# The low parts of weight blocks, formed by an accumulating DMA onto the negated high part

## The chip, the cores and the metric

The kernel runs on one core of one Trainium2 chip. The metric is the device time of one execution in microseconds (us); smaller is better. The engines are named as in the profile: PE (TensorE; PEld is its weight load), DVE (VectorE), ACT (ScalarE), POOL (GpSimd) and SP (SyncE, which issues most DMAs).

## The reference

One step of a two-layer streaming model, in float32, for a prompt of 512 tokens and a sample of 32 tokens, of width 1024. In both layers the normed input goes through `w_mix_in`; 256 of its columns query a memory of 256 rows, and the other 768 go through a state space mixer (S5, 48 groups of 64 states) in layer 0 and through latent attention with 12 heads in layer 1. Both parts go through `w_mix_out` and are added to the stream. A feed-forward part with a short convolution follows.

```python
for layer in range(DEPTH):                                     # DEPTH = 2
    z = rms_norm(h, norm_mix_g[layer]) @ w_mix_in[layer]
    z_mix, z_mem = z[..., :MIX_IN], z[..., MIX_IN:]            # 768 and 256 columns
    mem_out = memory_attend(rms_norm(z_mem...), mem_k[layer], mem_v[layer])
    mix_out = s5_mixer(z_mix, ...) if layer == 0 else mla_attention(...)
    h = h + concatenate([mix_out, mem_out]) @ w_mix_out[layer]
    h = h + conv_ffn(rms_norm(h, norm_ffn_g[layer]), ...)      # 1024 -> 5632 -> 2816 -> 1024
```

The memory's keys and values of the prompt are computed for both layers by `w_mem_kv` (`memory_kv`). The outputs are the stream, these keys and values, the new latents and rotary keys, and the final states of S5 and of the convolution.

## The kernel before, in words

The stream lies feature-major in `h[0..7]`, 128 features by 544 columns (512 of the prompt, 32 of the sample). Float32 products are made from float32r parts: an operand x is split into a high part `hi` (x rounded by a copy) and a low part `lo` = x - `hi`, and a product is `hi*hi + hi*lo + lo*hi`. `gemm` and `gemm_part` (L322) issue these three for a block of 128 output features, in two halves of 272 columns: 8 slices of 128 input features give 48 matmuls per block of 128x1024 weights, 6 slices give 36 per block of 128x768.

A weight block comes through `weights` (L227 to L233). SP loads it into `wraw` (L229), ACT copies it to `whi` (L230), and POOL subtracts into `wlo` (L231). Where a caller passes `lo_eng=V`, DVE subtracts: the four blocks of `mem_kv` for layer 1, and two of the three blocks of `kv_group`. `wraw`, `whi` and `wlo` have three buffers each, handed out in turn; the buffers of a block come back when PE has done its last matmul on it (`wfree`), and `wraw` when the low part is formed. So the high part of a block starts when PE ends the block three places earlier. 186 blocks come this way. The first two blocks of layer 0 (`weights_part`, L240) and the nine blocks of `w_uq` (L1284) make their low parts by code of their own.

The program runs in this order: the first product of layer 0 (`z0`) with the parameters of S5 (`s5_params`, L532 to L660); the S5 stage, six steps in which DVE and POOL form matrices (`s5_wv` L668 to L670, `s5_wc` L695 to L706), DVE scans (`s5_scan`, L761 to L779) and the eight blocks of `mem_kv` (matmuls at L348) go along as filling; the memory's attention and the gated product of layer 0; `mix_out`; `ffn` of layer 0; the same for layer 1 with the latent attention instead of S5. In `ffn` each pair of blocks gives two halves of the convolution: `conv` takes the product out of PSUM on DVE (L842 to L844), copies context columns on POOL (L846, L847), scales on ACT (L849) and adds on DVE (L850, L851). `down` multiplies back. Ahead of `ffn` and of layer 1 stands a norm: `norm_stat` sums squares on PE (L258, L260), `rsqrt` (L249 to L253) works on DVE, `norm_bcast` transposes on PE (L282).

A scheduler orders the instructions of each engine when the program is built, and engines run their own lists in order.

Of the kernel before, what the change touches and what calls it, by code (L numbers as in the profile page):

```python
# [9 lines left out]
F32 = mybir.dt.float32  # L10
F32R = mybir.dt.float32r
I32 = mybir.dt.int32
AF = mybir.ActivationFunctionType
ALU = mybir.AluOpType
# [47 lines left out]
# by how many instructions a unit moves ahead in the order of issue  # L62
# [15 lines left out]
class Slots:  # L78
    """Fixed buffers handed out in turn; the order of reuse is the order of the trace."""
# [38 lines left out]
    def retire(self, *tiles):  # L118
        """the buffers on these tiles are not handed out again"""
        self.gone |= {t[:].tensor.name for t in tiles}  # L120
        self.free = [t for t in self.free if t[:].tensor.name not in self.gone]
# [16 lines left out]
def body(ctx, tc, A, O):  # L138
# [29 lines left out]
    def sm(n, name, bufs=2):  # L168
        """small tiles: per name a ring of fixed buffers"""
        ring = small.setdefault((name, n), [[], 0])  # L170
        if len(ring[0]) < bufs:
            ring[0].append(base.tile([128, n], F32, name=f"{name}{n}_{len(ring[0])}"))
            return ring[0][-1]
        ring[1] += 1
        return ring[0][(ring[1] - 1) % bufs]

    # ---- constants and small parameters
# [36 lines left out]
    # ---- helpers  # L214
# [4 lines left out]
    def split_parts(po, smp):  # L219
        """high and low parts of a block given by its prompt and sample columns"""  # L220
        hi, lo = R.get(NT), R.get(NT)
        for c, x in ((slice(0, NP), po), (slice(S0, NT), smp)):
            S.activation(hi[:, c], x, AF.Copy)
            V.tensor_tensor(lo[:, c], x, hi[:, c].bitcast(F32), ALU.subtract)
        return hi, lo

    def weights(ap, *n, lo_eng=None):  # L227
        raw, hi, lo = WR.get(*n), WH.get(*n), WL.get(*n)
        nc.sync.dma_start(raw, ap)  # L229
        S.activation(hi, raw, AF.Copy)  # L230
        (lo_eng or P).tensor_tensor(lo, raw, hi.bitcast(F32), ALU.subtract)  # L231
        WR.put(raw)
        return hi, lo  # L233

    def weights_part(w, ap, c, lo_eng):
        """part of a weight block, ready on its own"""
        raw, hi, lo = (a[:, c] for a in w)
        nc.sync.dma_start(raw, ap[:, c])
        S.activation(hi, raw, AF.Copy)
        lo_eng.tensor_tensor(lo, raw, hi.bitcast(F32), ALU.subtract)  # L240
# [25 lines left out]
    def norm_stat(accs, bs):  # L266
        """1/rms per token from partial sums of squares [128, NT], tokens on the partitions"""
        ps = bs.get(512)
        if len(accs) == 2:
            V.tensor_tensor(accs[0], accs[0], accs[1], ALU.add)  # L270
        stat_cols(accs[0], ps)
        F.put(*accs)
        x = sm(5, "nx")
        V.tensor_scalar(x, ps[:, :5], 1.0 / D, EPS, ALU.mult, ALU.add)  # L274
        bs.put(ps)
        return rsqrt(x, 128, 5, "nr")

    def norm_bcast(r, bs):
        """the same along the columns on all partitions"""
        pa, pb = bs.get(512), bs.get(512)  # L280
        for t in range(4):
            T.transpose(pa[:, 128 * t:128 * t + 128], r[:, t:t + 1].to_broadcast([128, 128]), ident)  # L282
        T.transpose(pb[:, :NS], r[:NS, 4:5].to_broadcast([NS, 128]), ident[:NS, :NS])  # L283
        rb = F.get(NT)
        V.tensor_copy(rb[:, :NP], pa)
        V.tensor_copy(rb[:, S0:], pb[:, :NS])
        bs.put(pa, pb)
        return rb
# [21 lines left out]
    def gemm(ps, xs, w):  # L310
        """feature layout product of one block of 128 features: psum pair = w^T x"""
        for k in range(len(xs)):
            gemm_part(ps, xs, w, k, len(xs))
        wfree(w)
# [16 lines left out]
    # ---- memory keys and values of the prompt, both layers  # L331
# [85 lines left out]
    # ---- attention to the memory  # L417
    def mem_attend(l, zm, kv_p, kv_s, fm, bm, out):
# [25 lines left out]
        # sample: the 4 heads' queries side by side on the partitions  # L444
# [81 lines left out]
    # ---- S5: partitions hold two groups of 64 states (groups 8m+i and 8m+4+i), columns the 24 pairs  # L526
    NPR = 4 * NM

    def s5_exp(pool, x, name):
        """exp of a small tile to float32 accuracy"""  # L530
        k, r, y, e = (pool.tile([128, NPR], F32, name=f"{name}{i}") for i in "kry2")
        V.tensor_scalar(x, x, -87.0, 88.0, ALU.max, ALU.min)  # L532
        V.tensor_scalar(k, x, 1.0 / math.log(2.0), MAGIC, ALU.mult, ALU.add)
        V.tensor_scalar(k, k, MAGIC, None, ALU.subtract)
        V.scalar_tensor_tensor(r, k, -LN2_HI, x, ALU.mult, ALU.add)
        V.scalar_tensor_tensor(r, k, -LN2_LO, r, ALU.mult, ALU.add)
        V.tensor_scalar(e.bitcast(I32), k, 127.0, 8388608.0, ALU.add, ALU.mult)
        V.tensor_scalar(y, r, 1.0 / 5040, 1.0 / 720, ALU.mult, ALU.add)
        V.tensor_tensor(y, y, r, ALU.mult)
        for c in (120, 24, 6, 2, 1):  # L540
            V.scalar_tensor_tensor(y, y, 1.0 / c, r, ALU.add, ALU.mult)
        V.scalar_tensor_tensor(y, y, 1.0, e, ALU.add, ALU.mult)
        return y

    def s5_params(pool, tmp, sp5):
# [16 lines left out]
        # angles of the powers 1, 8, 16, ..., 512  # L562
# [28 lines left out]
        # input factor (lambda - 1) / a  # L591
# [16 lines left out]
        def cm(o, n, a, b):  # L608
            """powers o..o+n-1 = power a times powers b..b+n-1"""
# [10 lines left out]
        # b scaled by the input factor: -im, re, im  # L620
# [7 lines left out]
        # unit rotations by 8 theta at chunk positions 0..64, then 0..4 again  # L628
# [14 lines left out]
        # the same with the real and imaginary parts on the partitions  # L643
# [18 lines left out]
    def s5_wv(q, m, fs):  # L662
        """per group the map of a chunk's input to the state, [128 (step, channel), (re, im), pair, 128]"""
# [23 lines left out]
    def s5_wc(q, m, fs, bs):  # L687
        """per group the map of the state to the chunk's output, and the kernel within the chunk, written to DRAM"""
# [23 lines left out]
    def s5_kernel(q, m, fs):  # L712
        """the kernel within the chunk in its Toeplitz form"""
# [8 lines left out]
    def s5_input(zt, fs, bs):  # L722
        """zt [128, 552], tokens in chunks of 8 -> [128 (step, channel), 8 groups, 69 chunks], last step first"""
# [20 lines left out]
    def s5_scan(q, m, u, wv, fs, bs):  # L744
        """states before each chunk [128, (re, im), 4 pairs, 70]: 0..63 prompt, 64 its end, 65..68 sample, 69 its end.
        The state turns by 8 theta per chunk: in the turning frame both parts follow a real recurrence"""
# [63 lines left out]
    # ---- shared layer parts  # L810
    def mix_out(l, xs, rs, bs):
        """h += w_out^T xs; sums of squares for the next norm"""
# [94 lines left out]
    # ---- layer 0  # L907
# [11 lines left out]
    # the first two blocks part by part as their data comes in  # L919
# [83 lines left out]
    R, fx = slots(lr, 4, F32R, 512, "rb"), slots(lr, 14, F32, FW, "fx")  # L1003
# [5 lines left out]
    # units of the memory's keys and values that go along with each step  # L1009
# [100 lines left out]
    # ---- layer 1  # L1110
# [19 lines left out]
    # query latent (gain applied, scale deferred) and memory queries  # L1130
# [42 lines left out]
    # per column (4 tiles x 4 heads of the prompt, the sample) the scale of the query latent, its square over the widths  # L1173
# [6 lines left out]
    # latent and rotary key of the new tokens  # L1180
# [23 lines left out]
    def finish_latents():  # L1204
# [39 lines left out]
        # the rotary key, three times on the partitions: high, high, low parts  # L1244
# [28 lines left out]
    # queries: per group of 4 heads the projections, then norms, rotation and transposes  # L1273
# [82 lines left out]
    def absorb(g, qa):  # L1356
        """the sample's queries taken to the latent's side of the key projection; the rotary part high, low, high"""
# [18 lines left out]
    # norms of the keys of the cache and of the new tokens of the sample  # L1376
# [34 lines left out]
    # scores of the sample against all its keys, keys on the partitions, before the rotary part  # L1411
# [21 lines left out]
    def sample_attend(g):  # L1433
        """weights of the sample for four heads, the sum of its latents, the values from it"""
# [19 lines left out]
        # each part has its own maximum: factors that bring the parts together, over the sum  # L1454
# [43 lines left out]
    # keys and values of the prompt for a group  # L1498
# [49 lines left out]
    def prompt_scores(qt, kt):  # L1548
        """one head: weights, 4 query tiles in 3 buffers"""
# [20 lines left out]
    def prompt_values(prs, vt, h0, smp):  # L1570
        """the two heads of a pair side by side on the output's partitions"""
# [40 lines left out]
    def run(*gens):  # L1612
        """units of several streams in turn"""
        gens = list(gens)
        while gens:
            gens = [(k, g) for k, g in gens if unit(k, g) is not g]
# [44 lines left out]
    # how many units of the memory's attention go along with each round  # L1661
# [52 lines left out]
def arrays(a):  # L1714
# [44 lines left out]
    def pairs(v):  # L1759
        """[48 groups, 64 states, ...] -> [128 (half, state), 24 pairs, ...]"""  # L1760
        v = v.reshape((NM, 2, 4) + v.shape[1:])
        v = np.moveaxis(v, (1, 3), (0, 1))
        return v.reshape((128, 4 * NM) + v.shape[4:])
# [36 lines left out]
```

## Time and profile before

| | |
|---|---|
| median of 3 runs | 1480.92 us (1479.81 to 1484.13) |
| span of the profiled execution, first to last instruction | 1480.6 us |
| PE busy | 1411.5 us, 95% of the span |
| DVE busy | 876.6 us, 59% |
| ACT busy | 590.8 us, 40% |
| POOL busy | 711.6 us, 48% |
| moved by DMA | 120.49 MB, 81 GB/s on average |

The profiled execution has no separate time beside its span; the span lies 0.3 us under the median of the runs. Busy shares are averages over stages of different kinds, so the rows below are read by stage.

### The profile page before, as it was taken

What the parts mean: (1) busy time and instruction counts of PE and PEld (TensorE: products, weight loads), DVE (VectorE), ACT (ScalarE), POOL (GpSimd) and SP (SyncE); (2) the same over time, 40 slices, a digit from 0 to 9 for tenths busy, and PEclk for the clock granted to TensorE, in tenths of its full rate; (3) what the DMA queues carried; (4) which work ended last, traced back from release to release, by engine and by line L of the source; (5) the groups of instructions that cost most, each with busy time, mean ns of one, the idle gap of its engine ahead of it and who ended that gap; (6) DMA issues with size and microseconds to landing.
All of it is one profiled execution on the core that took longest, in us unless ns stands there. A gap on an engine that the chain in (4) does not pass through costs nothing. (4 is left out here: it accounts for less than half of the span.)

```text
span 1480.6 us, 26541 instructions
## 1 busy us (share of the span) xinstructions
PE 1411.5 (95%) x10693; PEld 1319.2 (89%) x10693; DVE 876.6 (59%) x1807; ACT 590.8 (40%) x1061; POOL 711.6 (48%) x643
## 2 busy tenths in 40 slices
PE   7686789989999999999999999999999999999998
PEld 6675678989999999999998998557999999999998
DVE  8999975177742773265447765673367633772462
ACT  5334455243432332244454554563334422442231
POOL 4647635545544554456636522442635544554442
PEclk9898899999999999999999999999989999999999
DMA  5222222212222222222223230000222222222222
GB/s 209 85 68 74 87 86 73 99 59 86 93 93 86 86 86 87 90 81 89 84 83 98 65 107 29 15 15 15 86 72 86 86 87 86 92 93 87 86 78 86
DMA packets 45115, 120.49 MB, mean 81 GB/s; under 512 B 5152, under 2 KB 14336, under 8 KB 44992
## 3 DMA queue, kind: packets, MB, share of 16 engines
q1 hardware_dynamic: 43008, 114.80, 23.1%
q10 hardware_dynamic: 1152, 2.10, 0.4%
q0 software_dynamic: 832, 1.91, 0.4%
q8 instruction: 84, 1.38, 0.4%
q14 instruction: 39, 0.32, 0.1%
HBM read 113.17 MB, written 5.61 MB: 80 GB/s over the span
## 5 line engine op out<-in xcount | busy, mean ns | idle before, releaser
L322 PE MATMUL bank<-rc,whi 128*128 128x272 f32 x3728 | 632.5, 291 | 5.0 <-DVE rc L303 4.2
L231 POOL TENSOR_TENSOR wlo<-wraw,whi 128x1024 fp32r<-128x1024 f32 (+2 forms) x180 | 421.4, 2341 | 373.8 <-ACT whi L230 368.8
L322 PEld LDWEIGHTS bank<-rc,whi 128*128 128x128 f32 x3728 | 532.8, 190 | 9.2 <-DVE rc L303 5.3
L322 PE MATMUL bank<-rc,wlo 128*128 128x272 f32 x1864 | 389.9, 290 | 0.0
L230 ACT ACTIVATE whi<-wraw 128x1024 fp32r<-128x1024 f32 (+2 forms) x186 | 191.2, 1028 | 411.5 <-PE bank L322 309.7
L322 PEld LDWEIGHTS bank<-rc,wlo 128*128 128x128 f32 x1864 | 294.8, 190 | 0.3 <-issue 0.2
L322 PE MATMUL bank<-g,whi 128*128 128x272 f32 x1408 | 235.2, 289 | 0.0
L850 DVE SCALAR_TENSOR_TENSOR fa<-fa,gp,fa 128x546 f32<-128x546 f32 x88 | 160.1, 1819 | 80.8 <-ACT fa L849 80.8
L322 PEld LDWEIGHTS bank<-g,whi 128*128 128x128 f32 x1408 | 199.3, 188 | 0.5 <-ACT g L216 0.3
L322 PE MATMUL bank<-g,wlo 128*128 128x272 f32 x704 | 146.2, 289 | 0.0
L864 DVE TENSOR_TENSOR h<-bank,h 128x272 f32<-128x272 f32 x96 | 37.8, 435 | 170.8 <-PE bank L322 170.8
L322 PEld LDWEIGHTS bank<-g,wlo 128*128 128x128 f32 x704 | 110.6, 188 | 0.0
L849 ACT ACTIVATE fa<-fa,gp 128x546 f32<-128x546 f32 x88 | 74.4, 845 | 48.2 <-DVE fa L844 48.2
L846 POOL COPY fa<-gp 128x2 f32<-128x2 f32 x88 | 18.6, 212 | 148.6 <-DVE g L217 106.2
L890 ACT ACTIVATE fa<-fa 128x546 f32<-128x546 f32 x44 | 29.1, 662 | 131.0 <-DVE fa L851 131.0
L851 DVE SCALAR_TENSOR_TENSOR fa<-fa,gp,fa 128x546 f32<-128x546 f32 x88 | 69.3, 788 | 3.1
L322 PE MATMUL bank<-ra,whi 128*128 128x272 f32 x256 | 52.3, 328 | 19.7 <-DVE fa L966 8.5
L322 PEld LDWEIGHTS bank<-ra,whi 128*128 128x128 f32 x256 | 43.0, 218 | 22.7 <-DVE fa L966 9.0
L847 POOL COPY fa<-fa 128x4 f32<-128x4 f32 x88 | 56.5, 642 | 11.7 <-DVE fa L844 11.7
L842 DVE TENSOR_TENSOR fa<-bank,fa 128x272 f32<-128x272 f32 x88 | 38.6, 438 | 33.6 <-PE bank L322 31.9
L217 DVE TENSOR_TENSOR g<-fa,g 128x544 fp32r<-128x544 f32 x44 | 37.8, 860 | 31.6 <-ACT g L216 31.6
L891 DVE TENSOR_TENSOR fa<-fa,fa 128x512 f32<-128x512 f32 x44 | 30.5, 693 | 35.1 <-ACT fa L890 35.1
(678 smaller groups left out, 2016.8 us busy)
## 6 DMA issues: line engine op xcount, KB each, us to landing
wraw<-i_w_f SPq DMA_DIRECT2D x120, 512.0 KB
wraw<-i_w_out SPq DMA_DIRECT2D x16, 512.0 KB
wraw<-i_w_in SPq DMA_DIRECT2D x14, 512.0 KB
wraw<-i_w_f SPq DMA_DIRECT2D x16, 384.0 KB
wraw<-i_w_mkv SPq DMA_DIRECT2D x8, 512.0 KB
wraw<-i_w_uq SPq DMA_DIRECT2D x9, 384.0 KB
wraw<-i_w_glu SPq DMA_DIRECT2D x6, 384.0 KB
h<-i_x SPq DMA_DIRECT2D x8, 272.0 KB
```

The costliest lines, as they stand in the source:

```text
L217: V.tensor_tensor(lo, src, hi.bitcast(F32), ALU.subtract)
L230: S.activation(hi, raw, AF.Copy)
L231: (lo_eng or P).tensor_tensor(lo, raw, hi.bitcast(F32), ALU.subtract)
L322: T.matmul(ps[q][:, :c], ww, xx[:, c0:c0 + c], start=k == 0 and i == 0, stop=k == n - 1 and i == 2)
L842: V.tensor_tensor(u[:, 2:274], ps[0][:, :272], rb[:, :272], ALU.mult)
L847: P.tensor_copy(view(cvo, [[2, 2], [1, 2]], 4 * c), view(u, [[34, 2], [1, 2]], 512))
L849: S.activation(y, u[:, 2:548], AF.Identity, scale=gcol("cw", 3 * ci + 2), bias=gcol("cb", ci))
L850: V.scalar_tensor_tensor(y, u[:, 1:547], gcol("cw", 3 * ci + 1), y, ALU.mult, ALU.add)
L851: V.scalar_tensor_tensor(y, u[:, 0:546], gcol("cw", 3 * ci), y, ALU.mult, ALU.add)
L864: V.tensor_tensor(h[m][:, c0:c0 + cc], ps[qd][:, :cc], h[m][:, c0:c0 + cc], ALU.add)
L890: S.activation(yg, yg, AF.Silu)
L891: V.tensor_tensor(u[:, 2:514], ya[:, :NP], yg[:, :NP], ALU.mult)
```

## The change

`weights` forms the low part in two steps. ACT writes the raw block times -1 into `wlo`, which rounds as the high part does, so that `wlo` = -`whi`. Then a DMA that POOL issues reads the block from DRAM a second time and adds it to `wlo` in SBUF. The subtraction on POOL or DVE is gone, and `lo_eng` has no effect. The raw buffer comes back after ACT's second copy. The pool `fx` of the S5 stage has 13 buffers in place of 14. Apart from comments that are taken out, nothing else is changed.

```diff
     def weights(ap, *n, lo_eng=None):
         raw, hi, lo = WR.get(*n), WH.get(*n), WL.get(*n)
         nc.sync.dma_start(raw, ap)
         S.activation(hi, raw, AF.Copy)
-        (lo_eng or P).tensor_tensor(lo, raw, hi.bitcast(F32), ALU.subtract)
+        S.activation(lo, raw, AF.Copy, scale=-1.0)
+        P.dma_start(lo, ap, accum_op=ALU.add)
         WR.put(raw)
         return hi, lo
...
-    R, fx = slots(lr, 4, F32R, 512, "rb"), slots(lr, 14, F32, FW, "fx")
+    R, fx = slots(lr, 4, F32R, 512, "rb"), slots(lr, 13, F32, FW, "fx")
```

Three places show how the engines' lists move. In the program of the change, lines behind `weights` stand two higher (L846 is L848 there), `whi` is written at L231, `wlo` at L232, and the accumulating DMA stands at L233. The names are the tiles of the code with a buffer number.

ACT in `ffn` of layer 0, before: one copy per block (L230) between the convolution's scaling (L849) and the gate (L890, L216).

```order
L849 ACTIVATE fa_83<-fa_77,gp 128x546
L890 ACTIVATE fa_83<-fa_83 128x546
L216 ACTIVATE g_2_2814<-fa_90 128x544
L230 ACTIVATE whi_97<-wraw_94 128x1024
L849 ACTIVATE fa_84<-fa_79,gp 128x546
L230 ACTIVATE whi_98<-wraw_95 128x1024
L849 ACTIVATE fa_85<-fa_89,gp 128x546
```

The same place on ACT with the change:

```order
L231 ACTIVATE whi_97<-wraw_94 128x1024
L232 ACTIVATE wlo_100<-wraw_94 128x1024
L851 ACTIVATE fa_88<-fa_91,gp 128x546
L892 ACTIVATE fa_88<-fa_88 128x546
L216 ACTIVATE g_6_2845<-fa_90 128x544
L231 ACTIVATE whi_98<-wraw_95 128x1024
L232 ACTIVATE wlo_101<-wraw_95 128x1024
```

The negated copy stands right behind the high part, ahead of the convolution's scaling.

POOL in `ffn` of layer 0, before: two subtractions per pair of blocks among the small copies of the convolution.

```order
L231 TENSOR_TENSOR wlo_99<-wraw_93,whi_96 128x1024
L847 COPY fa_74<-fa_90 128x4
L231 TENSOR_TENSOR wlo_100<-wraw_94,whi_97 128x1024
L847 COPY fa_74<-fa_77 128x4
L846 COPY fa_77<-gp 128x2
L846 COPY fa_90<-gp 128x2
```

The same place on POOL with the change:

```order
L233 DMA wlo_100<-i_w_f 128x1024
L849 COPY fa_76<-fa_89 128x4
L233 DMA wlo_101<-i_w_f 128x1024
L848 COPY fa_89<-gp 128x2
L848 COPY fa_73<-gp 128x2
L849 COPY fa_76<-fa_90 128x4
```

Each subtraction is replaced by a DMA issue; one small copy of a pair has moved ahead of the pair's first issue.

POOL at the start of the S5 stage, before: low parts of `w_in` blocks stand between the products for the S5 matrices.

```order
L231 TENSOR_TENSOR wlo_101<-wraw_95,whi_98 128x1024
L704 TENSOR_TENSOR fx_858<-cn,sp_145 128x32
L695 TENSOR_TENSOR fa_73<-cc_395,prd 128x576
L695 TENSOR_TENSOR fx_847<-cc_395,prd 128x576
L668 TENSOR_TENSOR fa_76<-bb_394,pi 128x512
L668 TENSOR_TENSOR fa_74<-bb_394,pr 128x512
L231 TENSOR_TENSOR wlo_99<-wraw_93,whi_96 128x1024
L670 TENSOR_TENSOR fa_74<-fa_74,fa_76 128x512
```

The same place on POOL with the change:

```order
L697 TENSOR_TENSOR fa_92<-cc_396,prd 128x576
L697 TENSOR_TENSOR fx_853<-cc_396,prd 128x576
L699 TENSOR_TENSOR fa_92<-fa_92,fx_853 128x576
L233 DMA wlo_99<-i_w_in 128x1024
L670 TENSOR_TENSOR fa_75<-bb_395,pi 128x512
L233 DMA wlo_100<-i_w_in 128x1024
L233 DMA wlo_101<-i_w_mkv 128x1024
L670 TENSOR_TENSOR big<-bb_395,pr 128x512
```

Several products now stand ahead of the low part of that `w_in` block; the products and the low parts are otherwise the same.

## Rows read from the trace of the kernel before

**Rows 1.** Windows by stage: length, busy us of each engine, granted PE clock, DMA.

```profile
core 0: us, PE busy (x) PEld busy (x) DVE busy (x) ACT busy (x) POOL busy (x), PEclk, DMA share, GB/s
...
37.00:185.00 148.00, 109.49 (x924) 93.71 (x923) 144.09 (x221) 62.41 (x142) 91.61 (x66) 0.89 0.25 78
185.00:260.00 75.00, 69.28 (x491) 60.82 (x490) 48.60 (x127) 42.15 (x102) 29.64 (x35) 0.96 0.26 81
260.00:740.00 480.00, 474.07 (x3761) 472.45 (x3760) 246.37 (x404) 171.80 (x217) 247.85 (x183) 1.00 0.25 86
```

**Rows 2.** The same windows, the instructions of L231 alone (DVE, then POOL).

```profile
37.00:185.00 148.00, 7.04 (x4) 22.47 (x9) 0.89 0.25 78
185.00:260.00 75.00, 0.00 (x0) 16.43 (x8) 0.96 0.26 81
```

**Rows 3.** Timeline of DVE in the S5 stage: start, length, engine, line.

```profile
40.99 2.01 DVE L616 TENSOR_TENSOR pi<-big 128x24 f32<-128x24 f32 x1
...
61.94 2.54 DVE L639 TENSOR_TENSOR big<-tab,p_sc 128x192 f32<-128x192 f32 x1
...
67.08 0.34 DVE L640 TENSOR_TENSOR tab<-big 128x192 f32<-128x192 f32 x1
...
120.12 0.43 DVE L762 TENSOR_TENSOR fx<-bank,tab 128x276 f32<-128x276 f32 x1
...
121.33 2.58 DVE L764 TENSOR_TENSOR big<-fx,fx 128x276 f32<-128x276 f32 x1
```

**Rows 4.** Timeline of POOL beside it.

```profile
61.77 2.50 POOL L231 TENSOR_TENSOR wlo<-wraw,whi 128x1024 fp32r<-128x1024 f32 x1
```

**Rows 5.** Timeline of PE in the S5 stage, first low part of a `mem_kv` block.

```profile
88.80 0.40 PE L348 MATMUL bank<-wlo,rb 128*128 128x512 f32 x1
```

**Rows 6.** Timeline of DVE and POOL at a norm, and L249 by itself (ns min/median/max).

```profile
1079.12 1.88 DVE L249 TENSOR_SCALAR nr<-nx 128x5 int32<-128x5 int32 x1
1078.62 2.35 POOL L231 TENSOR_TENSOR wlo<-wraw,whi 128x1024 fp32r<-128x1024 f32 x1 [2.38 <-ACT whi L230]
L249 DVE TENSOR_SCALAR nr<-nx x4: 164/2018/2157, 30.9 to 1079.1; 128x5 int32<-128x5 int32 x4
PE bank L282 <- DVE nr L253: 3.7, 2, 2.1
```

**Rows 7.** Timeline of ACT in `ffn` of layer 0, and in `down`.

```profile
406.40 1.06 ACT L230 ACTIVATE whi<-wraw 128x1024 fp32r<-128x1024 f32 x1 [2.36 <-PE bank L322]
413.55 1.05 ACT L230 ACTIVATE whi<-wraw 128x1024 fp32r<-128x1024 f32 x1
679.24 0.85 ACT L230 ACTIVATE whi<-wraw 128x768 fp32r<-128x768 f32 x1 [1.42 <-PE bank L322]
```

**Rows 8.** Timeline of PE: the first matmuls on those blocks and on their low parts.

```profile
418.46 0.66 PE L322 MATMUL bank<-g,whi 128*128 128x272 f32 x4
418.96 0.41 PE L322 MATMUL bank<-g,wlo 128*128 128x272 f32 x2
424.51 0.67 PE L322 MATMUL bank<-g,whi 128*128 128x272 f32 x4
425.02 0.41 PE L322 MATMUL bank<-g,wlo 128*128 128x272 f32 x2
686.56 0.42 PE L322 MATMUL bank<-g,wlo 128*128 128x272 f32 x2
```

**Rows 9.** DMA: queue with packets, MB, share; a POOL issue, KB, us to landing.

```profile
q1 hardware_dynamic: 43008, 114.80, 23.1%
o_mem_v<-fa POOLq DMA_DIRECT2D x1, 256.0 KB, 2.6
194.90 0.73 POOL L380 DMA_DIRECT2D o_mem_v<-fa  x1
```

**Rows 10.** Groups by line: count, busy us, mean ns, idle time before.

```profile
L850 DVE SCALAR_TENSOR_TENSOR fa<-fa,gp,fa 128x546 f32<-128x546 f32 x88 | 160.1, 1819 | 80.8 <-ACT fa L849 80.8
L851 DVE SCALAR_TENSOR_TENSOR fa<-fa,gp,fa 128x546 f32<-128x546 f32 x88 | 69.3, 788 | 3.1
```

## The prediction

> **What bounds the kernel now.** I read the windows by stage first, because the page's 95% for PE is a mean. From 260 us on PE is busy for 474.07 of 480 us and is the bound; DVE, ACT and POOL work about half the time there [rows 1]. Between 37 and 185 us, in the S5 stage, it is the other way: DVE is busy for 144.09 of 148 us, PE for 109.49, at a granted clock of 0.89. So work taken from DVE shortens the S5 stage, and work taken from POOL or given to ACT counts in the later stages only if PE comes to wait for it. The second view is the timeline of DVE beside POOL. While POOL subtracts a low part from 61.77 us for 2.50 us [rows 4], DVE's L639 on 128x192 takes 2.54 us; L640 of the same width takes 0.34 us later [rows 3]. So a DVE instruction with two operands in SBUF stands still until POOL's subtraction has ended. The third view is the time between a block's high part and PE's first use of its low part, which says how late a low part may come.
>
> The Trainium skill ("SBUF — State Buffer", section "Who interferes with whom") says that such an instruction shares its second read path with GpSimd and that the one that issues second is blocked for the whole of the other; the trace agrees with its 2.54 us against 0.34.
>
> **The change, part by part.**
>
> *The S5 stage, 37 to 185 us.* Two things leave DVE. Its own four subtractions cost 7.04 us [rows 2]. And POOL's nine, 22.47 us [rows 2], stop blocking DVE. In the timeline six DVE instructions stand still beside them, from L616 at 40.99 us (2.01 us for 24 columns) to L764 at 121.33 us (2.58 us, where L762 of that width takes 0.43) [rows 3]. I take 2.0 us for each (2.54 - 0.34 and 2.58 - 0.43 are 2.2, L616 is 1.8 above its like): 12 us. DVE's work falls by 19 us. Not all of it will show. PE's 109.49 us must fit into what is left, ACT gets some thirteen more copies of 1.06 us [rows 7] on 62.41, and POOL's other products still block DVE. The lists are dealt out anew with one `fx` buffer less, which can add waits. I take three quarters, 14 us; the bounds are 0 (all is lost to new waits) and 19.
>
> *185 to 260 us.* POOL's eight subtractions, 16.43 us [rows 2], block short chains of the memory's attention and the gated product. PE is idle for only 5.7 us of the 75 [rows 1], so I take 2 us, between 0 and 5.
>
> *The norms ahead of `ffn` and of layer 1.* PE waits there for a chain of small DVE instructions. L249 on 128x5 takes 1.88 us beside a subtraction on POOL, and 0.164 us undisturbed; its median is 2.018 us over four [rows 6]. Three of the four are disturbed, and PE waits for what follows (L282 for L253) [rows 6]. That is 1.7 to 2.0 us three times, 5.6 us; I take 5, since ACT's extra copy may lengthen other links. Bounds 0 and 6.
>
> *The steady stretch, PE bound.* DVE gets faster here too (L850 takes 1819 ns, its sister L851 on the same shape 788 [rows 10]), which is worth nothing as DVE is not waited for. The question is whether low parts still come in time. ACT's high part starts at 406.40 us, when PE has let the buffer go, and PE first needs the low part at 418.96 [rows 7, 8]. Now ACT needs 1.06 us twice, and the DMA has the rest: 418.96 - 406.40 - 2.12 - 0.1 for the handover = 10.3 us. For the pair's other block it is 425.02 - 413.55 - 2.2 = 9.3 us. The tightest is a 128x768 block of `down`: 686.56 - 679.24 - 1.8 = 5.5 us.
>
> No row shows an accumulating DMA. A plain one from POOL of 256 KB takes 2.6 us from issue to landing, 0.73 us of it on POOL [rows 9]; queue 1 moves 114.80 MB in 23.1% of the span, so 512 KB (0.524 MB) in 1.56 us of all 16 engines [rows 9]. A plain copy of 512 KB would thus land after 2.6 + 0.8 = 3.4 us: the lower bound. The accumulation must read the block and also what it adds to. If reading, reading back and writing each cost a pass one after another, it takes three passes: 4.7 us of the engines, landing after 6.5 us. That is my upper bound. I take two passes, since a plain copy already reads and writes in one: 3.1 us of the engines, landing after 5.0 us, or 6.5 us if the next raw block shares the engines. All of it is below 9.3. For 384 KB it is 2.6 + 0.4 + 1.2 = 4.2 us, 5.4 us when shared, against 5.5. The engines' load per block of 424.51 - 418.46 = 6.05 us [rows 8] rises from 1.56 to 4.7 us, 78%. So I cost the steady stretch at nothing, with 1 us for `down` and the start. The cover is thin: it is gone at 2.9 passes ((6.05 - 1.56) / 1.56).
>
> The Trainium skill ("Collectives: The Full Stack", section "The bandwidth ceiling: the fold count and why AG ≠ RS ≠ AR") says that the add in the DMA path costs no time itself but needs two source reads, and so halves the rate. By it the sum would be that of the two passes; no run here shows it yet.
>
> POOL's queue: an issue of some 0.73 us takes the place of 2.50 us [rows 4, 9]. It starts one ACT copy later, so the copies behind it (L846, L847) are reached no later than now. Queued behind ACT's new copy is the convolution's scaling, later by 1.06 us, and behind that DVE's L850, which gains 1.03 us [rows 10]. SP's raw loads are freed earlier, not later. In the S5 stage low parts have ample time: the first `mem_kv` low part is formed from 66.8 us on and used at 88.80 [rows 5].
>
> **Sum.** 14 + 2 + 5 - 1 = 20 us off the profiled span of 1480.6, and the median of the runs lies 0.3 us above it: 1461 us. A measurement of this kernel can tell about 0.3% (4.4 us) from no change.
>
> **The rivals.**
>
> *The engines' DMA rate becomes the bound (slower).* It decides from 2.9 passes on. At three, a block needs 1.56 + 4.68 = 6.24 us, 0.19 more than PE, over the 150 blocks of 128x1024 that go through `gemm` by way of `weights`: 28 us, less the 20 gained, 1489 us. At four passes it is 7.8 us, 1.75 more per block: 262 us, less 20, some 1720 us. For it: nothing here shows the operation. Against: 78% by the two passes, and DMA share 0.25 now [rows 1]. Chance 0.17, some 0.11 of it above 1500 us.
>
> *Low parts come late without a full DMA queue (slower).* A landing of 11 us instead of 5 would stretch two blocks (12.1 us, plus the 0.5 us before the first low part is used) to 13.2 us, 0.3 us per block, 45 us in all: 1507 us. It would need twice the 5.0 us worked out. Chance 0.04.
>
> *The S5 stage gives nothing (no change).* DVE's time is freed, but the new order with 13 buffers, ACT's copies or PE's own chain take its place, and POOL's issues hold up the norms as the subtractions did. Then 1478 us. For it: PE and POOL are not far behind DVE there, 109.49 and 91.61 us with waits on each other [rows 1]. Chance 0.13. A reordering that loses 5 to 15 us is a variant: 1490 us, chance 0.05.
>
> **How the numbers follow.** Forecast 0.61, no gain 0.13, DMA rate 0.17, lateness 0.04, bad order 0.05. The forecast alone spans 1446 (19 + 5 + 6, and some 4 beyond, as products on POOL start earlier) to 1476. The range runs to 1500, so that it holds the no-gain case, three passes and the bad order; outside are 0.15 above and 0.04 below. Faster is 0.61, the same 0.13, slower 0.26.
>
> **What would show it.** L231's subtractions on POOL and DVE gone, 186 more copies on ACT. In the S5 stage no DVE instruction of 24 to 276 columns over 2 us beside a low part, DVE busy about 125 us in a stage some 14 us shorter. L249 at 0.16 us at all three norms. From the end of the S5 stage on, PE's blocks at 6.05 us as now, and PE never waiting for the accumulating DMA. The software queue's packets at twice a plain packet's time. I am wrong if PE's weight loads wait for `wlo` in `ffn`, if DMA's share goes to 0.9 or more there, or if the S5 stage keeps its length with DVE idle in it.

## The result, and the profile after

The changed kernel takes 1460.3 us, the median of 4 runs (1459.68 to 1460.44), against 1480.4 us for the kernel before in the same comparison (1479.77 to 1484.13): 20.1 us less, a ratio of 0.9854 with a 95% interval of 0.9842 to 0.9867. The profiled execution took 1460.42 us, its span 1458.6 us. 1461 was forecast. The median came within 1 us of it, but the terms did not. Even the sum is less close than it looks: in the runs of both kernels that list the two, the time lies 1.7 to 1.8 us above the span (1460.42 against 1458.6 here), not 0.3, so the profiled execution before, with its span of 1480.6 us, was some 2 us slower than the median of its kernel. In spans 20 us less were forecast, and it is 22.0.

The windows by stage, as in [rows 1]:

```profile
core 0: us, PE busy (x) PEld busy (x) DVE busy (x) ACT busy (x) POOL busy (x), PEclk, DMA share, GB/s
37.00:185.00 148.00, 124.97 (x1012) 107.17 (x1012) 137.98 (x248) 79.24 (x171) 80.59 (x77) 0.87 0.58 135
185.00:260.00 75.00, 72.87 (x538) 65.16 (x537) 31.05 (x91) 47.49 (x99) 22.24 (x36) 1.00 0.60 136
260.00:740.00 480.00, 479.91 (x3821) 478.51 (x3820) 202.91 (x416) 249.72 (x312) 110.78 (x187) 1.00 0.80 172
```

PE does more in each window, and from 260 to 740 us it is idle for only 0.1 us. DMA share there is 0.80, which is the 78% that was worked out. DVE's and POOL's work is down, ACT's is up.

The page's DMA queues and issues (the last number is us from issue to landing), and two groups by line:

```profile
q0 software_dynamic: 27616, 96.16, 37.5%
q1 hardware_dynamic: 43008, 114.80, 27.1%
...
wlo<-i_w_f POOLq DMA_DIRECT2D x120, 512.0 KB, 7.3
...
wlo<-i_w_f POOLq DMA_DIRECT2D x16, 384.0 KB, 6.1
```

```profile
L233 POOL DMA_DIRECT2D wlo<-i_w_f x136 | 117.3, 863 | 304.9 <-ACT wlo L232 303.0 <-ACT fa L851 1.9
...
L852 DVE SCALAR_TENSOR_TENSOR fa<-fa,gp,fa 128x546 f32<-128x546 f32 x88 | 69.4, 789 | 139.4 <-ACT fa L851 139.4
```

The accumulating queue takes 37.5% of 1458.6 us for 96.16 MB, so 2.98 us of 16 engines per 512 KB (3.1 was forecast). The raw load has gone from 1.56 to 1.80 us (27.1% of 1458.6 us, 114.80 MB). L852 was L850 before and took 1819 ns [rows 10]; now it takes as long as its sister.

To see where the 22 us of span were won, I took PE's first matmul of each stage from the timelines and subtracted. The table says how much longer (+) or shorter (-) each stretch is than in the kernel before; three experiments, told below, stand beside the change.

| stretch (us, against before) | change | 13 buffers alone | DMA in S5 only | DMA at norms only |
|---|---|---|---|---|
| start to third `w_in` block | -4.1 | +0.7 | -2.5 | -0.2 |
| to the end of `w_in` | -1.1 | +3.8 | -2.4 | +3.4 |
| to the gated product | -9.1 | +3.9 | -9.9 | +3.7 |
| gated product, `mix_out` | -1.2 | +2.4 | -0.2 | +0.7 |
| norm: first two blocks of `ffn` 0 | -5.8 | +1.2 | 0.0 | -5.8 |
| rest of `ffn` 0 | +0.6 | -0.8 | +0.6 | -0.8 |
| norm: first two blocks of layer 1 | -1.7 | 0.0 | +1.5 | 0.0 |
| rest of `w_in`, attention | +5.1 | -0.1 | +0.6 | +1.5 |
| `mix_out` of layer 1 | -0.1 | -0.1 | 0.0 | -0.1 |
| norm: first two blocks of `ffn` 1 | -6.8 | -2.3 | -2.3 | -6.8 |
| rest | +2.3 | -0.6 | -0.5 | -0.6 |
| sum | -22.0 | +8.3 | -15.1 | -5.0 |

So the start and the S5 stage give 14.3 us, the norms 14.4, and the attention stage and the ends of the `ffn` parts cost 8. Small entries have to be read with care: the kernels of e9 and e12 below form the blocks of the start as the change does, and yet reach the end of `w_in` 4 us later than it.

**S5 stage.** DVE's timeline of the changed kernel, the instructions of [rows 3] (L616 is L618 now, L639 is L641, L764 is L766):

```profile
32.36 0.17 DVE L618 TENSOR_TENSOR pi<-big 128x24 f32<-128x24 f32 x1
...
58.90 0.35 DVE L641 TENSOR_TENSOR big<-tab,p_sc 128x192 f32<-128x192 f32 x1
...
116.83 0.49 DVE L766 TENSOR_TENSOR big<-big,fx 128x276 f32<-128x276 f32 x1
```

All three stood 2 us or more before. POOL's own products still hold DVE up: L641 on 96 columns takes 1.45 us at 53.58 us, beside a product of L699 that POOL runs from 53.51 us for 1.41. Between the same two marks, the end of `w_in` and the gated product, both kernels do the same work; the windows of before, then of after:

```profile
87.40:207.30 119.90, 90.27 (x794) 72.71 (x791) 115.92 (x195) 58.66 (x142) 72.39 (x57) 0.91 0.30 93
```

```profile
82.20:193.00 110.80, 94.73 (x793) 76.65 (x791) 100.84 (x186) 65.09 (x150) 57.53 (x57) 0.86 0.55 134
```

DVE is busy for 15.1 us less, and the stretch is 9.1 us shorter. PE takes 4.5 us more for the same matmuls, at a granted clock of 0.86 instead of 0.91.

**A norm.** The windows of the first two blocks of `ffn` 0 (marks are PE's first matmuls), before:

```profile
301.46:311.29 9.83, 7.61 (x66) 7.14 (x65) 7.31 (x8) 4.14 (x6) 4.79 (x2) 1.00 0.20 65
311.29:322.03 10.74, 8.67 (x61) 8.24 (x54) 6.96 (x18) 0.84 (x2) 2.57 (x2) 0.84 0.15 50
```

and after:

```profile
285.97:293.48 7.51, 7.51 (x66) 7.14 (x64) 5.80 (x8) 5.24 (x8) 2.62 (x2) 1.00 0.50 103
293.48:300.72 7.24, 7.15 (x61) 6.72 (x54) 5.00 (x18) 1.80 (x4) 1.05 (x2) 1.00 1.01 233
```

Three things went. In the first block PE was idle for 2.22 us, in the second for 2.07, and in the second it ran at a granted clock of 0.84. PE's timeline of before shows what it waited for:

```profile
306.33 0.52 PE L322 MATMUL bank<-rc,whi 128*128 128x272 f32 x2 [1.45 <-DVE rc L303]
...
308.13 0.52 PE L322 MATMUL bank<-rc,whi 128*128 128x272 f32 x2 [0.78 <-DVE rc L303]
...
315.63 0.65 PE L282 MATMUL bank<-cn,nr 128*128 128x128 f32 x4 [2.07 <-DVE nr L253]
...
316.75 0.96 PE L322 MATMUL bank<-rc,whi 128*128 128x272 f32 x4
...
317.96 1.11 PE L322 MATMUL bank<-rc,whi 128*128 128x272 f32 x4
```

The same four matmuls take 0.66 us after the change (at 296.96 us); in before they take up to 1.11 behind the 2.07 us wait, at a mean granted clock of 0.72 from 316 to 322 us. L303 forms the low part of the normed input, and L249 begins the square root; by themselves (ns min/median/max), L303 of before, then L305 and L251 of after, which are the same instructions:

```profile
L303 DVE SCALAR_TENSOR_TENSOR rc<-h,gp,rc x32: 768/1123/2909, 297.7 to 1075.4; 128x544 fp32r<-128x544 f32 x32
```

```profile
L305 DVE SCALAR_TENSOR_TENSOR rc<-h,gp,rc x32: 770/784/1936, 283.2 to 1055.1; 128x544 fp32r<-128x544 f32 x32
```

```profile
L251 DVE TENSOR_SCALAR nr<-nx x4: 161/171/172, 27.1 to 1059.0; 128x5 int32<-128x5 int32 x4
```

L303 was held up by two things: by L231's subtraction (2.20 us at 304.08, beside a subtraction from 302.70 to 305.70), and by POOL's own squares of the norm, L296, which came behind that subtraction (1.87 us at 306.21, beside L296 from 305.66 to 307.49).

At the norm ahead of `ffn` 1 the clock counts for most. The second of its two blocks, before and after:

```profile
1078.78:1090.12 11.34, 11.26 (x61) 10.54 (x55) 6.69 (x18) 0.85 (x2) 2.38 (x2) 0.58 0.13 48
```

```profile
1058.60:1065.87 7.27, 7.18 (x61) 6.74 (x55) 4.99 (x18) 1.82 (x3) 1.05 (x2) 1.00 1.00 233
```

PE was busy all the time with the same matmuls, at a granted clock of 0.58. L249 stood still there for 1.88 us [rows 6], but PE did not wait for it, since its matmuls lasted that much longer. Over the six blocks of the three norms, 7.6 of the 14.4 us are idle time of PE that has gone, and 6.8 are busy time: the same matmuls at a higher granted clock.

**What was lost.** PE's waits for the accumulating DMA in the whole execution, three in all:

```profile
PE bank L324 <- DMA wlo<-i_w_in: 2.9, 1, 2.9
...
PE bank L1192 <- DMA wlo<-i_w_dkv: 1.8, 1, 1.8
PE bank L324 <- DMA wlo<-i_w_f: 1.6, 1, 1.6
```

They end at 30.09 us, at 745.83 us (the three `w_dkv` blocks, needed together) and at 1431.37 us (the last `down`).

### The profile page after: what moved, and what is told of

Read it like the earlier page. It is cut to its first block, busy times and chain, and to the rows that moved or that the text cites. A ratio compares the mean times of both kernels' runs of the same rounds, so it can differ in the third digit from the quotient of the medians.

```text
span 1458.6 us, 26919 instructions
## 1 busy us (share of the span) xinstructions
PE 1409.9 (97%) x10693; PEld 1315.7 (90%) x10693; DVE 738.8 (51%) x1801; ACT 753.4 (52%) x1247; POOL 408.7 (28%) x649
## 3 DMA queue, kind: packets, MB, share of 16 engines
q0 software_dynamic: 27616, 96.16, 37.5%
q1 hardware_dynamic: 43008, 114.80, 27.1%
## 4 chain that ended last, share of the span: by engine, by line
PE 82%; DVE 2%; issue 1%; ACT 1%; DMA 1%; POOL 0%; DVEq 0%; POOLq 0%; ACTq 0%
PE bank L324 65%; PE bank L1309 2%; PE bank L1557 2%; PE bank L1396 2%; PE bank L1593 1%; PE bank L1510 1%; PE bank L1484 1%; PE bank L1582 1%; PE bank L1192 1%; PE bank L482 1%; PE bank L520 1%; PE bank L1424 1%; DMA wlo<-i_w_f 0%; PE bank L510 0%; PE bank L1365 0%
## 5 line engine op out<-in xcount | busy, mean ns | idle before, releaser
L231 ACT ACTIVATE whi<-wraw 128x1024 fp32r<-128x1024 f32 (+2 forms) x186 | 191.1, 1028 | 360.6 <-issue 314.2
L233 POOL DMA_DIRECT2D wlo<-i_w_f x136 | 117.3, 863 | 304.9 <-ACT wlo L232 303.0
L232 ACT ACTIVATE wlo<-wraw 128x1024 fp32r<-128x1024 f32 (+2 forms) x186 | 189.0, 1016 | 9.9 <-PE bank L350 9.3
L852 DVE SCALAR_TENSOR_TENSOR fa<-fa,gp,fa 128x546 f32<-128x546 f32 x88 | 69.4, 789 | 139.4 <-ACT fa L851 139.4
L866 DVE TENSOR_TENSOR h<-bank,h 128x272 f32<-128x272 f32 x96 | 38.2, 435 | 173.0 <-PE bank L324 172.4
L853 DVE SCALAR_TENSOR_TENSOR fa<-fa,gp,fa 128x546 f32<-128x546 f32 x88 | 69.4, 789 | 3.1
L848 POOL COPY fa<-gp 128x2 f32<-128x2 f32 x88 | 19.0, 220 | 169.4 <-DVE g L217 105.1
L849 POOL COPY fa<-fa 128x4 f32<-128x4 f32 x88 | 18.0, 204 | 166.5 <-DVE fa L846 166.5
L216 ACT ACTIVATE g<-fa 128x544 fp32r<-128x544 f32 x44 | 28.9, 658 | 37.3 <-DVE fa L894 37.3
```

Source lines behind the costliest of these rows:

```text
L232: S.activation(lo, raw, AF.Copy, scale=-1.0)
L233: P.dma_start(lo, ap, accum_op=ALU.add)
L852: V.scalar_tensor_tensor(y, u[:, 1:547], gcol("cw", 3 * ci + 1), y, ALU.mult, ALU.add)
L853: V.scalar_tensor_tensor(y, u[:, 0:546], gcol("cw", 3 * ci), y, ALU.mult, ALU.add)
L866: V.tensor_tensor(h[m][:, c0:c0 + cc], ps[qd][:, :cc], h[m][:, c0:c0 + cc], ALU.add)
```

## The experiments

**Theory A** is the prediction's: POOL's subtraction holds up DVE's instructions, and what goes is these stalls, with DVE's own subtractions. **Theory B**: the lists dealt out anew, with 13 buffers, make the S5 stage shorter. **Theory C**: low parts were late behind POOL's subtraction, or only DVE's own subtractions counted. A second dispute is whether the DMA engines' rate is the limit that the prediction's cover assumed.

**13 buffers alone (e1).**

```diff
-    R, fx = slots(lr, 4, F32R, 512, "rb"), slots(lr, 14, F32, FW, "fx")
+    R, fx = slots(lr, 4, F32R, 512, "rb"), slots(lr, 13, F32, FW, "fx")
```

> The kernel before with 13 fx buffers in place of 14 and nothing else. Theory A (what goes is GpSimd's hold on two-operand DVE instructions, and DVE's own four subtractions): no gain, 1478 to 1485 us, and POOL's subtractions still hold up L616, L639 and L764 for about 2 us each. Theory B (the lists dealt out anew with 13 buffers make the S5 stage shorter): 1465 to 1472 us, with the gated product starting near 193 us as after the change.

1488.9 us, ratio 1.0045 (1.0026 to 1.0065), so some 6 us slower by the medians. Theory B falls: the buffer that the change gives up, with the order that follows from it, costs 10.8 us up to the first `ffn` block in this profile (table). The ten times spread from 1482.7 to 1491.9 us, and the profile is of one of 1490.7; the third experiment, whose kernel subtracts in the same way up to `mix_out`, loses 7.6 us up to the same mark. It is a loss that the change carries and covers. From these two kernels to the change the mark moves from 312.26 and 309.02 to 285.97 us: with equal buffers the DMA is worth 23 to 26 us there. Between the end of `w_in` and the gated product DVE is as busy here as before (116.4 us), while PE needs 98.6 us instead of 90.3 for the same matmuls, at a granted clock of 0.85; why was not tried. The change with 14 buffers was not run.

**The DMA in the S5 stage only (e2), at the norms only (e3).** In both the choice stands at the call:

```diff
+        if acc:
+            S.activation(lo, raw, AF.Copy, scale=-1.0)
+            P.dma_start(lo, ap, accum_op=ALU.add)
+        else:
+            (lo_eng or P).tensor_tensor(lo, raw, hi.bitcast(F32), ALU.subtract)
```

with `acc` set for `w_in` of layer 0, `w_mkv` and `w_glu` in the first, and around the three norms in the second.

> The changed kernel, where only w_in of layer 0, w_mkv and w_glu go by the accumulating DMA; mix_out, ffn and all of layer 1 subtract on POOL or DVE as before. Theory A: the gated product ends about 14.5 us earlier than before and everything behind it stays as before, so 1480.4 - 14.5 = 1466 us. If the gains of the S5 stage came from elsewhere, or the later norms were changed by the order of the earlier stages, it lies below 1462 or above 1472 us.

1468.1 us, ratio 0.9910 (0.9885 to 0.9935): 14.4 us off the 1482.5 us of before on this chip, as theory A says. The two blocks ahead of `ffn` 0 keep their old length, those of layer 1 take 1.5 us more, and those of `ffn` 1 2.3 us less, as with 13 buffers alone (table).

> Only 26 of the 186 blocks go by the accumulating DMA: the last three of each mix_out, the first four of each ffn, the last three of ffn 0 and the first three of w_in of layer 1, so those that stand around the three norms; 13 fx buffers. Theory A as read from the trace after: the norms ahead of both ffn parts give 5.8 and 6.8 us, that ahead of layer 1 1.9 us, so 14.5 us off what 13 buffers alone give, 1466 us. By the term of the prediction it would be 5 us, 1475 us. If a norm is held up by something else than the blocks beside it, nothing, 1480 us.

The blocks are 20, not the 26 that this text counts. 1477.1 us, ratio 0.9964 (0.9952 to 0.9975), where 1466 was expected; that figure started from 1480 us, without the price of the buffer. Against 13 buffers alone, the fair yardstick, it is 11.8 us less. The norms of both `ffn` parts reach exactly the length that they have in the whole change, 5.8 and 6.8 us under before. Against 13 buffers alone that is 7.0 and 4.5 us: at `ffn` 1 that kernel is 2.3 us shorter than before with much the same waits for L303 (2.1 us), since its second block ran at a granted clock of 0.82, not 0.58. The norm of layer 1 gains nothing, and DVE's and POOL's timelines say why: the block subtracted there is the fourth of `w_in`, which the edit left out.

```profile
717.20 2.18 DVE L254 TENSOR_SCALAR nr<-nx 128x5 int32<-128x5 int32 x1
```

```profile
716.94 2.41 POOL L236 TENSOR_TENSOR wlo<-wraw,whi 128x1024 fp32r<-128x1024 f32 x1 [2.58 <-ACT whi L231]
```

So at this norm it is the one subtraction beside the chain that decides, not the number of them.

**An idle POOL instruction given back, with two operands (e4) and with one (e5).** Behind the DMA issue stands a result that nobody reads:

```diff
         P.dma_start(lo, ap, accum_op=ALU.add)
+        P.tensor_tensor(raw, raw, hi.bitcast(F32), ALU.subtract)      # e4
+        P.tensor_scalar(raw, raw, 1.0, 0.0, ALU.mult, ALU.add)        # e5
```

> The changed kernel, and behind each accumulating DMA POOL subtracts the high part from the raw block in place: nobody reads the result, but POOL again spends some 2.4 us on an instruction with two SBUF operands per block, and the raw buffer comes back later. The low parts are as in the changed kernel. Theory A (POOL's two-operand instruction holds up DVE's): the gains at the norms go (5.8 + 6.8 + 1.9 us) and in the S5 stage some 10 us go, so 1475 to 1490 us, with L251 (the first step of rsqrt) near 2 us again in most of its four. Theory C (it was the low part's own lateness behind POOL's subtraction, or DVE's own subtractions): 1460 to 1466 us.

> As the run with the idle subtraction, but POOL's idle instruction has one SBUF operand (the raw block times 1, in place). If what holds DVE up is that two operands of POOL and two of DVE are read together, theory A gives no loss: 1460 to 1466 us, and L251 stays at 0.16 us. If POOL's time in SBUF of any kind does it, or POOL's queue being late with its next DMA, the loss is its share of the run with the subtraction, by its length.

e4 takes 1632.9 us (ratio 1.1037, 1.0995 to 1.1079), e5 1483.4 us (1.0008, 0.9992 to 1.0024). The groups of e4, then of e5 (mean ns after the busy time):

```profile
L234 POOL TENSOR_TENSOR wraw<-wraw,whi 128x1024 f32<-128x1024 f32 (+2 forms) x186 | 486.3, 2617 | 26.3 <-ACT wlo L232 25.9 <-ACT whi L231 0.4
...
L853 DVE SCALAR_TENSOR_TENSOR fa<-fa,gp,fa 128x546 f32<-128x546 f32 x88 | 282.5, 3210 | 105.0 <-ACT fa L852 105.0
```

```profile
L234 POOL TENSOR_SCALAR wraw<-wraw 128x1024 f32<-128x1024 f32 (+2 forms) x186 | 245.3, 1319 | 28.9 <-ACT wlo L232 28.5 <-ACT whi L231 0.4
...
L853 DVE SCALAR_TENSOR_TENSOR fa<-fa,gp,fa 128x546 f32<-128x546 f32 x88 | 174.0, 1977 | 108.9 <-ACT fa L852 108.9
```

L853 is the L852 of the change, 789 ns there. It grows by 2.42 us beside an instruction of 2.62, and by 1.19 beside one of 1.32. At a norm of e5, a link of 0.17 us of the square root takes 1.70 beside POOL's idle instruction (DVE, then POOL; both end at 311.7 us, though by the profile POOL's starts 0.3 us later):

```profile
310.02 1.70 DVE L256 SCALAR_TENSOR_TENSOR nr<-nre,nr 128x5 f32<-128x5 f32 x1
```

```profile
310.33 1.37 POOL L234 TENSOR_SCALAR wraw<-wraw 128x1024 f32<-128x1024 f32 x1
```

DVE has the same instructions as in the change, and e5's DMAs land no later (5.6 us after issue), so theory C falls and A's core stands: holding up DVE is what costs. But the form of it that e5 was to test, that POOL too must read two operands, is wrong. One is enough, and the price goes with POOL's length: against the change, the start and the way to the gated product lose 26.4 us in e4 and 13.8 in e5, the three norms 22.1 and 9.0. Between the end of `w_in` and the gated product alone DVE is busy for 13.3 and 5.2 us more, and the stretch is 10.5 and 4.0 us longer. POOL's own products and the raw buffers come later in both runs too; what part of the loss is theirs was not separated. The Trainium skill ("SBUF — State Buffer", section "Who interferes with whom") has it so: a DVE instruction with two SBUF inputs contends with any GpSimd instruction that reads SBUF. These two runs agree, with the 1.19 and 2.42 us above.

e4 loses another 59.6 us in `ffn` 0 and 58 us behind the second one's norm, which I had not expected. ACT's gate (L893) waits for the stalled DVE chain, 184 us in all (71 in the change), and the next blocks' copies stand behind it in ACT's list. So, as I read the lists, the negated copies are late, and PE waits 71.8 us for `wlo` in 37 waits. That is the prediction's second rival, lateness, with a DMA share of 0.65 from 260 to 740 us, but by a late start: the landing itself takes 5.5 us. The slack of the low parts is real, and a stall of 2.4 us twice per pair uses it up.

**How full the DMA engines may be (e6, e7, e10, e11, e12).** For each block of `w_f1` and `w_f2` SP moves further bytes to a scratch in DRAM that nobody reads: from the input in e6 and e7, from the raw buffer in e10 to e12.

```diff
         P.dma_start(lo, ap, accum_op=ALU.add)
+        nc.sync.dma_start(next(spare)[:, :n], ap[:, :n])      # e7; e6: half of it
+        nc.sync.dma_start(next(spare)[:, :n], raw[:, :n])     # e10; e11: half; e12: twice
```

> The changed kernel, and for each block of w_f1 and w_f2 SP also copies half of the block (256 KB) in DRAM to a scratch that nobody reads. Load of the DMA engines per 128x1024 block: 1.80 for the raw load (27.1% of 1458.6 us over 114.8 MB), 3.02 for the accumulation, 0.8 to 0.9 for this: 5.7 us of 6.05. The prediction's cover holds: within 4 us of 1460 us. If it was already used up, or landing times rather than the rate decide, it is slower by more than 10 us.

> The same with the whole block (512 KB, for w_f2 384 or 512 KB): load 4.82 + 1.6 to 1.8 = 6.4 to 6.6 us per block of 6.05 us. If the rate of the DMA engines becomes the bound from 6.05 us on, some 0.35 to 0.55 us per block over 136 blocks: 1505 to 1535 us, with PE waiting for wlo in ffn and DMA share near 1. If the engines are not the limit, 1460 us.

1477.4 us (ratio 0.9963, 0.9941 to 0.9986) and 1498.9 us (1.0117, 1.0081 to 1.0153). Neither tests what it was to test: as the copies depend on nothing, SP ran ahead, and all of them were over by some 300 us in e6 and some 450 us in e7. e6 loses its time there, 9.8 us against the change between the gated product and `ffn` 0, at a DMA share of 1.02 from 185 to 300 us. e7 still shows a saturated stretch and a free one of the same `ffn`:

```profile
316.60:430.00 113.40, 100.31 (x765) 98.00 (x764) 50.21 (x105) 55.14 (x65) 20.30 (x48) 0.98 1.03 347
480.00:650.00 170.00, 170.00 (x1353) 170.00 (x1353) 65.44 (x138) 80.81 (x93) 31.16 (x66) 1.00 0.79 174
```

So I tied the bytes to the raw block, with the change itself once more beside them.

> The changed kernel once more, as the yardstick on the chip of the three runs beside it: 1458 to 1463 us.

> The changed kernel, and for each block of w_f1 and w_f2 SP also writes the raw block out to a scratch in DRAM that nobody reads, 512 KB (384 for the short ones); it can't run ahead, since it needs the raw block. Load of the DMA engines 4.82 us + 1.6 to 1.8 = 6.4 to 6.6 us per block of 6.05 us. Rate theory: 0.35 to 0.55 us more per block over 136 blocks, 1505 to 1535 us, with DMA share near 1 in both ffn parts and PE waiting for wlo. Latency theory (only landing times count): under 1470 us.

> The same with half of each block, 256 KB: load 5.6 to 5.7 us of 6.05 us. Rate theory: within 4 us of the changed kernel, DMA share some 0.93 in ffn. If landing times stretch before the engines are full and PE already waits for wlo, 1470 us or more.

> As the run that writes each raw block of w_f1 and w_f2 out to a scratch, but twice. That run's writes added 7.9% of 16 engines, 0.88 us per 512 KB, and brought DMA share in ffn from 0.80 to 0.96 at 2 us per ffn. Twice that is 4.82 + 1.77 = 6.6 us, or by the shares 1.12 x 6.05 = 6.8 us, per block of 6.05 us. Rate theory: 0.5 to 0.75 us per block over 136 blocks, 1530 to 1565 us, with DMA share near 1. If PE still takes 6.05 us per block, it is not the engines' rate that sets the limit.

The changed kernel 1462.8 us (ratio 0.9891, 0.9843 to 0.9939), e11 1462.1 (0.9885, 0.9855 to 0.9915), e10 1465.1 (0.9907, 0.9874 to 0.9941), e12 1669.4 (1.1255, 1.1195 to 1.1316). The windows of `ffn` 0 in the change, e11, e10 and e12, in this order:

```profile
300.00:680.00 380.00, 380.00 (x3017) 379.73 (x3016) 164.08 (x331) 191.89 (x228) 77.45 (x153) 1.00 0.80 172
```

```profile
300.00:680.00 380.00, 379.13 (x3007) 378.63 (x3006) 163.06 (x329) 190.83 (x226) 77.59 (x153) 1.00 0.85 214
```

```profile
300.00:680.00 380.00, 378.94 (x3003) 378.23 (x3002) 162.63 (x329) 190.86 (x226) 77.58 (x153) 1.00 0.96 256
```

```profile
300.00:680.00 380.00, 329.27 (x2422) 320.44 (x2422) 119.88 (x258) 146.54 (x167) 55.60 (x118) 0.96 0.97 272
```

PE's row counts its matmuls: 3017, 3007 and 3003 in 380 us, then 2422. e10's queue 1, then PE's wait in e12:

```profile
q1 hardware_dynamic: 62592, 184.01, 35.0%
```

```profile
PE bank L330 <- DMA wlo<-i_w_f: 134.5, 83, 4.2
```

My size for e10 was wrong: a write from SBUF to DRAM costs 0.88 us of the engines per 512 KB there (queue 1 goes from 27.1% to 35.0%), not 1.6 to 1.8, so e10 fills the engines to 0.96 and not beyond, and costs at most 2 us per `ffn`. Twice as much asks for 6.6 us or more per block of 6.05, and then PE is the one that waits: 134.5 us for `wlo` in 83 waits, and some 100 us more per `ffn`. The rate theory holds, and the edge lies between these two. e12 is slower than the 1530 to 1565 us expected: a block takes 7.63 us (48 of 2138 matmuls in the 340 us from 320 us on). At a share of 0.97 that is 7.4 us of the engines per block, not 6.6 to 6.8, so the engines are full and a write costs them more than in e10. Why was not taken apart; the raw buffers are also held until their writes end.

**`w_dkv` by DVE's subtraction (e9).**

```diff
-    wk = [weights(A["w_dkv"]..., kn * 288)
+    wk = [weights(A["w_dkv"]..., kn * 288, lo_eng=V, acc=False)
```

> The changed kernel, where the three blocks of w_dkv subtract on DVE and do not go by the accumulating DMA. The attention stage lost 5 us against the kernel before; if 1.8 us of it is PE's wait for the last w_dkv block and some 1.5 us the lower clock that follows, 3 to 4 us come back, 1456 to 1458 us. If the loss is the order of the lists there, 1460 us.

1456.5 us (ratio 0.9848, 0.9817 to 0.9879). Against the change run beside it the rest of `w_in` and the attention are 5.9 us shorter: PE's wait for `w_dkv` (3.3 us in that run) is gone, and the granted clock in the stretch up to 760 us is 1.00 instead of 0.91. The windows of the change beside it, then of e9:

```profile
740.00:760.00 20.00, 16.75 (x121) 16.20 (x121) 6.71 (x24) 6.92 (x26) 1.46 (x2) 0.91 0.32 87
```

```profile
744.00:760.00 16.00, 16.00 (x129) 15.46 (x128) 7.52 (x25) 7.21 (x26) 0.73 (x2) 1.00 0.28 91
```

At 820 to 840 us the clock is also 0.91 where the change beside it has 0.83, which adds to the gain. But the first 85 us, which the edit does not touch, came out 4 us longer in this profile, and the ratios' intervals overlap. So the place of the loss is shown; that this version is faster than the change is likely, not settled.

## Why the prediction came out right, step by step

**"I take three quarters, 14 us" (S5 stage).** Start and S5 stage gave 14.3 us, but 4.1 of it ahead of 31 us, where the sum had put a loss with `down`. The S5 stage proper gave 10.2, inside the bounds of 0 and 19. DVE's busy time fell by 15.1 us from the end of `w_in` to the gated product, and by 21.2 from the third `w_in` block on, where 19 was forecast: about half of it showed, not three quarters. The order's price, which I named as waits that one buffer less "can add", is 7.6 to 10.8 us by e3 and e1; what the DMA saves is that much larger than the term. So the term's size, near 14, is luck, and its mechanism is right.

**"185 to 260 us": 2 us.** Gated product and `mix_out` gave 1.2.

**"The norms": 5 us, bounds 0 and 6.** This term failed: 14.4 us. I priced one instruction, L249, and not the chain around it. I also counted its stall three times, while the row of PE's waits has two of them, 3.7 us in all [rows 6]; at `ffn` 1 PE did not wait for it. PE also waited for L303, held up as told above, 2.2 us ahead of `ffn` 0 and 2.0 ahead of `ffn` 1. And around these waits the clock was lower, which I had put at nothing: at `ffn` 0 PE was busy for 8.67 us instead of 7.15 in the second block, at `ffn` 1 for 11.26 instead of 7.18. e3 shows that with the blocks beside the chain changed, both `ffn` norms have the length of the whole change; 2.3 us of the 6.8 at `ffn` 1 are a difference of the clock that 13 buffers alone show as well.

**"I cost the steady stretch at nothing, with 1 us for `down` and the start."** Right for PE's blocks in `ffn`, which stay at 6.05 us (2381 matmuls of `gemm` in the 300 us from 300 us on, 48 a block). `down` lost 1.6 us to one wait. PE "never waiting for the accumulating DMA", one of the signs named, did not come true: there are three waits, 6.3 us in all, and at the one in `down` PE's weight load waited for `wlo`, which had been named as a sign of being wrong. It stayed at one. The attention stage was not looked at, and lost 5.1 us: some 2 to the three `w_dkv` blocks that PE needs together, so that no block's time lies ahead of the last one, some 1.5 to 2 to the clock at 758 to 778 us (0.91), the rest late in the stage to the order of PE's list, which was only read and not tried.

**"Two passes", 3.1 us, landing 5.0 or 6.5 us.** 2.98 us; landing at 7.3 us (the median), later than either, though below the 9.3 that decides. For the 384 KB blocks of `down` it is 6.1 us, above the slack of 5.5 that was worked out; but the room there was larger: from the DMA's issue to PE's first use the median of these 16 blocks is 8.6 us. e10 and e11 landed at 5.6 and 5.5 us with more bytes to move, so the engines' mean load does not explain the 7.3. The traces point at the next raw load: in the change SP issues it 0.27 us ahead of the accumulating DMA, while in e4, e5, e10 and e11, which all hold the raw buffer longer and all land at 5.5 to 5.6 us, it is issued 1.9 to 3.3 us behind (medians). So 5.6 without and 7.3 with the raw load beside it, where I had 5.0 and 6.5; no run was made to test this. POOL's issue takes 0.86 us, not 0.73. The Trainium skill ("Collectives: The Full Stack", section "The bandwidth ceiling: the fold count and why AG ≠ RS ≠ AR") has the add read two sources and so halve the rate: 2.98 us against 1.56 for the plain load of before agrees, against 1.80 beside it less so, and 3.09 against 1.48 in e5 (38.2% and 21.9% of 1484.4 us) agrees again.

**The rivals.** The rate as the bound did not come, and e12 shows that it was a real danger: the change runs at a share of 0.80, 0.96 is nearly free, and a demand beyond full is 200 us slower. That the S5 stage gives nothing is refuted by e2. The bad order is there, but covered.

So the forecast came near because the norms' extra 9 us met an attention loss and other ends of about the same size, and the median came nearer still because the step from span to median was 0.3 us in place of 1.8. The direction followed from the right mechanism; the nearness was luck.

## What to carry to other kernels

In these runs an instruction on POOL that reads SBUF cost a DVE instruction with two operands beside it nearly its own length (1.19 of 1.32 us, 2.42 of 2.62). Look for it where PE waits for a short chain of small DVE instructions, and price the whole chain, with the lower clock around the wait, rather than one link. A transfer can take over such work while the DMA engines stay below full and each block has another block's time ahead of it; where PE needs several blocks at once, as with `w_dkv`, look whether the subtraction is better kept. Cost a buffer that a change gives up by itself: here it was 7.6 to 10.8 us beside the 20 that the change won.

## What was not expected of the hardware

One operand on POOL is enough to hold DVE up (1.37 us made a 0.17 us link 1.70). A write of 512 KB from SBUF to DRAM took 0.88 us of the 16 engines in e10 (more in e12), a load 1.48 to 1.80, an accumulation 2.98. L249, with five columns and a single tensor operand, stood still too, 1.88 us against 0.16 [rows 6], not only instructions with two.
